# Way down of a SwiGLU block: sums moved from GpSimd to VectorE, seven block products in another order, one operand prepared earlier, LayerNorm rows without GpSimd sums

## The chip, the cores and the metric

The kernel runs on one core of one Trainium2 chip. The metric is the device time of one execution in microseconds; the time before is the median of three runs, 1489.16 us (1487.93 to 1490.58). About 0.2% of it, 3 us, is what such a measurement can tell apart.

## The reference

One encoder layer on x of 1024 tokens by 1024 channels, in float32. A projection gives q, k and v of two attention branches (eight heads each of width 64) and two gates; the branches are projected, gated, summed and projected again, and a LayerNorm follows. What the change touches is the end:

```
x   = layer_norm(ALPHA * x + mix, ln1_g, ln1_b)
gu  = x @ w_ffn_in                 # 1024 x 5632: halves g and u of 2816 columns
g,u = split(gu)
ffn = (silu(g) * u) @ w_ffn_out    # the way up gives h = silu(g)*u, 1024 x 2816; this is the way down
x   = layer_norm(ALPHA * x + ffn, ln2_g, ln2_b)
```

layer_norm takes mean and variance over the 1024 channels of a token and applies gain and bias.

## The kernel before, in words

**Arithmetic.** Every float32 operand of a matmul is split in a high part (rounded to the format that TensorE takes, a ScalarE copy, line 106) and a low part (the rest, a VectorE subtract, line 107); a product is three matmuls: high by high, high by low, low by high (`mm3`, `product`, `triple`).

**Seven products.** Both ways of the feed-forward block use the Strassen-Winograd scheme: an operand is cut in 2 x 2 blocks, and seven block products replace eight, at the price of sums of blocks. On the way up a block of columns f (22 of them, 128 columns each of g and u) takes seven products of 12 matmuls, 84 in all, in the order 1, 2, 6, 5, 7, 3, 4 (`pair_steps`). A product that continues another is accumulated onto the same PSUM bank after ScalarE has copied what stood there (lines 185, 194, 198).

**The way up's last steps.** `up_steps` takes the results: `gt` is the tile with the gate half "11" and the half "22", `h` is the tile of the block's result. Line 846 and 851 apply Silu, 848 and 852 multiply. After an odd block, `left_sums` forms the left operands of the way down for the pair (f-1, f): four sums on GpSimd (lines 821 to 824), and seven stores of 128 x 512 to scratch in HBM (`left_dr`, line 827).

**The way down.** For each of the seven products (the order is in `ORDER`) there are 11 steps, one for each pair; a step loads a left operand (`load`, line 905), splits it (`split_left`), splits a right operand from the rows of w_ffn_out (`split_right`), and runs 12 matmuls, three on each of four banks (`triple`, line 945). The right operands that are sums of blocks are formed in place by `right_sums`, on GpSimd (lines 912, 915, 916, 918). `feed` asks for loads nine steps ahead, sums four ahead, splits three ahead. Two sets of four banks alternate: X (three tr and pv) and Z (two mm, two sc). After a product's last step `take` adds its banks to the accumulators `acc_t` on VectorE (lines 951, 953), which start from x1 (loaded at line 977). Product 4 comes last and runs bank by bank, so that one row of 128 tokens after the other is done; its left and right operands are split during product 3.

**The last LayerNorm.** `end_row` calls `layer_norm` for 128 tokens: statistics (744, 745), variance plus epsilon (746), the power -1/2 on GpSimd (747), centring and gain on VectorE (748). Then, where `quick` is false, ScalarE scales (755) and GpSimd adds the bias (756); where it is true, VectorE does both in two halves (751). Of the last LayerNorm only row 7 is quick. The result goes out by line 957.

**What sets the order.** The source gives an order of emission. The framework's planner places every engine's instructions at build time: an instruction goes onto its engine's queue when, by the planner's estimate, its operands and a buffer are ready, the earlier emitted first among those that are ready. Engines then run their queues in that order and wait for each other by semaphores. Nearly all DMAs are issued on SP's queue. Buffers of 128 x 1024 come from tags with a fixed number of slots (`SLOTS`): yt has 3 (gate tiles, h of odd blocks and of blocks 0 and 2), bw 9 (h of later even blocks, weights, later rows of w_ffn_out), op 8, gt 3 (weights and, on the way down, left operands two to a slot), kp and pt 4 each, xt 16, and qs, kh, kl, v two each, taken in turn (`QKV`). A new tile takes any slot of its tag that is free in the plan, and waits if there is none.

Of the kernel before, what the change touches and what calls it, by code (L numbers as in the profile page):

```python
# [11 lines left out]
F32 = mybir.dt.float32  # L12
# [6 lines left out]
P = 128  # L19
# [9 lines left out]
ORDER = (1, 2, 6, 5, 7, 3, 4)  # L29
# [3 lines left out]
HW = 512  # L33
# [15 lines left out]
def hybrid_trunk_kernel(ctx: ExitStack, tc, x, xt, w_in, b_gate, rel_bias, w_proj,  # L49
# [51 lines left out]
    left_dr = {(p, i): dr.tile([P, HW], F32, name=f"left_dr{p}_{i}")  # L101
# [714 lines left out]
    def left_sums(i):  # L816

        ha, hb = h_of.pop(2 * i), h_of.pop(2 * i + 1)
        sa, sb = slot("op", f"sa{i}"), slot("op", f"sb{i}")
        add = nc.gpsimd.tensor_tensor  # L820
        add(sb[:, LO], ha[:, LO], ha[:, HI], ALU.subtract)  # L821
        add(sa[:, LO], ha[:, HI], hb[:, HI], ALU.add)  # L822
        add(sa[:, HI], sa[:, LO], ha[:, LO], ALU.subtract)
        add(sb[:, HI], hb[:, LO], sa[:, HI], ALU.subtract)
        for p, t in ((1, ha[:, LO]), (2, hb[:, LO]), (4, hb[:, HI]), (5, sa[:, LO]),
                     (6, sa[:, HI]), (7, sb[:, LO]), (3, sb[:, HI])):
            dma(left_dr[p, i], t)

    def up_steps(f):
# [14 lines left out]
        def done(name, acc):  # L844
# [4 lines left out]
            elif name == "21":  # L849
# [3 lines left out]
                if f % 2:  # L853
                    left_sums(f // 2)
# [36 lines left out]
    raw_l, t2, ops = {}, {}, {}  # L891
    xbank, zbank = [], []
# [5 lines left out]
    def load(s):  # L898
        p, i = steps[s]
        if p in (1, 2):  # L900
            load_rows(p - 1, i)
# [5 lines left out]
    def right_sums(s):  # L907
        p, i = steps[s]
        tt = nc.gpsimd.tensor_tensor
        a, b = rows[0][i], rows[1][i]  # L910
        if p == 2:
            tt(a[:, LO], a[:, HI], a[:, LO], ALU.subtract)
        elif p == 6:
            t = t2[i] = slot("kp", f"t2_{i}")[:, LO]
            tt(t, b[:, HI], a[:, LO], ALU.subtract)
            tt(b[:, LO], b[:, LO], t, ALU.subtract)
        elif p == 5:
            tt(a[:, HI], b[:, HI], a[:, HI], ALU.subtract)

    first_tags = iter([("kp",)] * 4)  # L920
    wide = iter([("pt",)] * 4 + [("kp",)] * 4 + [("bw",)] * 3)
# [6 lines left out]
    def split_left(s):  # L928
        p, i = steps[s]
        tags = next(wide) if p == 4 else next(first_tags, QKV)  # L930
        ops["l", s] = split_to(tags, f"dl{p}_{i}", raw_l.pop((p, i)))

    def split_right(s):
        p, i = steps[s]
        a, b = rows[0][i], rows[1][i]
        src = {1: lambda: a[:, LO], 2: lambda: b[:, LO], 6: lambda: t2.pop(i), 5: lambda: a[:, LO],
               7: lambda: a[:, HI], 3: lambda: b[:, HI], 4: lambda: b[:, LO]}[p]()
        tags = ("xt",) if p == 4 else next(first_tags, QKV)
# [103 lines left out]
```

## Time and profile before

| what | value |
|---|---|
| median of the runs | 1489.16 us (1487.93 to 1490.58) |
| profiled execution, its own time | 1487.28 us |
| its span, first to last instruction | 1485.5 us |
| granted TensorE clock | 0.994 |
| way up, matmuls of line 168 | 822.6 to 1255.9 us |
| way down, matmuls of line 945 | 1255.8 to 1471.6 us |
| last store ends | 1485.5 us |

In the profile PE is TensorE's matmuls, PEld its weight loads, DVE is VectorE, ACT ScalarE, POOL GpSimd, SP the queue that issues DMAs. A row of a timeline gives the start, the duration, the engine, the line, what is written and read, how many instructions are merged, and in brackets the idle time of that engine just before and what ended it. A row of groups gives the busy time, the mean nanoseconds of one, then the idle time before them.

### The profile page before, as it was taken

The page shows a single profiled execution, that of the slowest core. Times are in us where ns is not written, and L with a number is a line of the kernel's source. Part 1 is how long each engine was busy: PE and PEld are TensorE (multiplying, and loading weights), DVE is VectorE, ACT ScalarE, POOL GpSimd, SP SyncE. Part 2 cuts the span into 40 slices and gives each one's busy share as a digit, 9 for nine tenths or more (in the row PEclk, how much of TensorE's full clock was granted, in tenths as well). Part 3 has the DMA queues.
Part 4 walks back from the last instruction along what each step waited for, and adds up shares of the span by engine and source line. Part 5 has one row for each costly group of instructions (what it writes and reads, how often), then busy time and mean ns, then how long its engine had stood idle before and what let it go on. Part 6 is the DMA issues. An engine that isn't in the chain of part 4 may idle for free.

```text
span 1485.5 us, 19020 instructions
## 1 busy us (share of the span) xinstructions
PE 1434.5 (97%) x6728; PEld 1176.0 (79%) x6728; DVE 997.1 (67%) x1575; ACT 689.2 (46%) x1222; POOL 391.3 (26%) x384
## 2 busy tenths in 40 slices
PE   8999999999999999999999799999999999999996
PEld 6788888887777888777888588888888888778875
DVE  8865556277677767786948976555555544796757
ACT  6444444376676666864403443333333332434532
POOL 0000000243346546850004121111111113771007
PEclk9999999999999999999999999999999999999998
DMA  6555544756554355748601143333222227843232
GB/s 213 158 183 171 170 149 162 228 167 174 156 156 129 125 145 177 218 168 278 223 15 72 57 140 129 107 106 101 98 91 98 101 101 255 327 134 120 93 100 113
DMA packets 75167, 219.41 MB, mean 148 GB/s; under 512 B 9392, under 2 KB 9392, under 8 KB 75072
## 3 DMA queue, kind: packets, MB, share of 16 engines
q1 hardware_dynamic: 75072, 218.19, 45.4%
q8 instruction: 53, 0.87, 0.2%
q14 instruction: 42, 0.34, 0.1%
HBM read 149.71 MB, written 68.45 MB: 147 GB/s over the span
## 4 chain that ended last, share of the span: by engine, by line
PE 72%; DVE 11%; DMA 5%; POOL 4%; issue 4%; ACT 3%; SPq 1%; DVEq 0%; POOLq 0%; ACTq 0%
PE sxf L168 14%; PE dn L945 10%; PE sxp L168 9%; PE szf L168 7%; PE gps L415 6%; PE szp L168 5%; PE syf L168 3%; PE syp L168 2%; PE ops L116 2%; PE ops L114 2%; PE tp_b L553 2%; PE ops L113 2%; PE yAps L603 2%; DVE kp_b L530 1%; PE tp_a L553 1%
## 5 line engine op out<-in xcount | busy, mean ns | idle before, releaser
L945 PE MATMUL dn<-dr,dl 128*128 128x512 f32 x924 | 213.0, 391 | 2.8 <-DVE dl L107 1.8
L945 PEld LDWEIGHTS dn<-dr,dl 128*128 128x128 f32 x924 | 172.3, 188 | 43.4 <-DVE dl L107 4.6
L532 POOL TENSOR_TENSOR w_b<-w_b,kp_b 128x511 f32<-128x511 f32 (+3 forms) x96 | 99.3, 1039 | 61.6 <-DVE kp_b L530 37.0
L107 DVE TENSOR_TENSOR dl<-raw,dl 128x512 fp32r<-128x512 f32 x77 | 68.7, 904 | 33.6 <-ACT dl L106 33.3
L106 ACT CAST dl<-raw 128x512 fp32r<-128x512 f32 x77 | 47.3, 623 | 83.4 <-PE dn L945 67.2
L747 POOL TENSOR_TENSOR mv<-mv,neghalf 128x1 f32<-128x1 f32 x16 | 23.3, 1454 | 237.2 <-DVE mv L746 233.2
L530 DVE TENSOR_TENSOR_SCAN kp_b<-kp_b,ident_ps 128x384 f32<-128x384 f32 (+6 forms) x88 | 78.5, 892 | 4.6
L415 PE MATMUL gps<-xh,wl_g 128*128 128x512 f32 x192 | 80.3, 418 | 0.0
L415 PE MATMUL gps<-xh,wh_g 128*128 128x512 f32 x192 | 80.3, 418 | 0.0
L415 PE MATMUL gps<-xl,wh_g 128*128 128x512 f32 x192 | 80.3, 418 | 0.0
L476 POOL MEMSET bias<- 64x64 f32 x8 | 1.2, 146 | 275.2 <-ACT bias L475 275.2
L821 POOL TENSOR_TENSOR sb<-h 128x512 f32<-128x512 f32 x11 | 18.9, 1720 | 205.1 <-PE syf L168 131.6
L497 POOL TENSOR_SCALAR w_a<-w_a,st_a 128x640 f32<-128x640 f32 (+2 forms) x64 | 46.4, 728 | 81.8 <-DVE st_a L496 69.0
L522 ACT ACTIVATE kp_b<-sc_b 128x512 f32<-128x512 f32 (+3 forms) x96 | 48.3, 503 | 42.1 <-PE sc_b L459 33.4
L107 DVE TENSOR_TENSOR dr<-rows,dr 128x512 fp32r<-128x512 f32 x66 | 55.4, 847 | 16.1 <-ACT dr L106 16.0
L107 DVE TENSOR_TENSOR pt_b<-tp_b,pt_b 128x512 fp32r<-128x512 f32 (+1 forms) x96 | 51.1, 542 | 17.6 <-ACT pt_b L106 17.4
L168 PE MATMUL szf<-x1S63h,wcf 128*128 128x512 f32 x176 | 57.8, 389 | 0.0
L106 ACT CAST pt_b<-tp_b 128x512 fp32r<-128x512 f32 (+1 forms) x96 | 47.7, 497 | 21.2 <-PE tp_b L553 21.1
L822 POOL TENSOR_TENSOR sa<-h,h 128x512 f32<-128x512 f32 x11 | 17.5, 1589 | 145.0 <-PE sxf L168 105.5
L106 ACT CAST pt_a<-tp_a 128x512 fp32r<-128x512 f32 (+1 forms) x96 | 40.4, 424 | 27.2 <-PE tp_a L553 26.5
L494 ACT ACTIVATE w_a<-w_a,st_a 128x640 f32<-128x640 f32 (+2 forms) x64 | 44.6, 699 | 17.2 <-DVE st_a L489 16.4
L553 PE MATMUL tp_b<-ident,w_b 128*128 128x128 f32 x288 | 48.2, 274 | 4.1 <-DVE pt_b L107 1.8
(1541 smaller groups left out, 4276.7 us busy)
## 6 DMA issues: line engine op xcount, KB each, us to landing
raw<-left_dr SPq DMA_DIRECT2D x77, 256.0 KB, 2.9
wLf<-in_w_ffn_in_dram SPq DMA_DIRECT2D x22, 512.0 KB, 3.8
wRf<-in_w_ffn_in_dram SPq DMA_DIRECT2D x22, 512.0 KB, 4.2
rows<-in_w_ffn_out_dram SPq DMA_DIRECT2D x22, 512.0 KB, 6.7
left_dr<-h SPq DMA_DIRECT2D x33, 256.0 KB, 2.0
v_dr<-v SPq DMA_DIRECT2D x16, 512.0 KB, 3.5
kl<-k_dr SPq DMA_DIRECT2D x32, 256.0 KB, 6.1
v<-v_dr SPq DMA_DIRECT2D x16, 512.0 KB, 3.3
```

Of the source, the lines that this page charges most:

```text
L106: nc.scalar.copy(dst_h, src)
L107: nc.vector.tensor_tensor(dst_l, src, dst_h.bitcast(F32), ALU.subtract)
L113: mm(acc, lh, rh, start=(i == 0), stop=False)
L168: mm(acc, lw[:, ks], rx, start=(first and kt == i == 0), stop=(kt == 3 and i == 2), skip_group_check=not first)
L415: mm(acc, lw[:, ks], rx[k][:, cs], start=(k == j == 0), stop=(k == KT - 1 and j == 2))
L494: nc.scalar.activation(s[:, 0:w], s[:, 0:w], AF.Exp, bias=st[:, m:m + 1], scale=-1.0, accum_out=st[:, 2:3])
L497: nc.gpsimd.tensor_scalar(s[:, 0:w], s[:, 0:w], st[:, 3:4], 0.0, ALU.mult, ALU.add)
L522: nc.scalar.activation(kp[:, c0:e], sc[:, 0:n], AF.Sigmoid, scale=-1.0)
L530: nc.vector.tensor_tensor_scan(kp[:, s0:e], kp[:, s0:e], ident_ps()[:, 0:e - s0], kp[:, s0 - 1:s0], ALU.mult, ALU.bypass)
L532: nc.gpsimd.tensor_tensor(be[:, m0:e], be[:, m0:e], kp[:, m0 - 1:e - 1], ALU.mult)
L553: tr(tp[:, (qb - lo_q) * P:(qb - lo_q + 1) * P], wt[qb - q0][:, (kb - qb) * P:(kb - qb + 1) * P], ident)
L945: mm(acc, lw, rx, start=(first and n == 0), stop=(last and n == 2), skip_group_check=steps[s][0] not in (1, 2, 5))
```

## The change

Four things change in the way down, and one at the end of each pair of blocks on the way up.

- The order of products becomes 5, 1, 3, 6, 2, 7, 4. Products 5, 1 and 2 begin fresh banks; 3 continues 5's banks, 6 continues 1's, 7 continues 6's and 4 continues 7's. Products 5, 3 and 2 use the first set (tr, tr, tr, pv), products 1, 6, 7 and 4 the second (mm, mm, sc, sc).
- The right sums are formed by VectorE in place: one for product 5, two for product 3 and one (`last_sum`) for product 4, emitted during product 2. Before, GpSimd formed four, for products 2, 6 and 5.
- The left operand of product 4 is split at the end of the way up: ScalarE copies the high part into the lower half of the odd block's gate tile, GpSimd subtracts, writing the low part over the value in the tile h; both halves are stored, and the way down loads them as one tile of 128 x 1024 (`load_last`, during product 6) that needs no split. The right operand of product 4 is split during product 7.
- Every row of the last LayerNorm is quick. Rows 0 and 1 are emitted during product 7 (steps 6 and 9), rows 2 and 3 during the first two quarters of product 4, rows 4 to 7 after their quarter as before.
- The takes of a product are emitted one for each of the steps 1 to 4 of the next product instead of all at its end; the loads of x1 are emitted at step 4 of the first product instead of ahead of it; the first operands use the tags of QKV and not kp.

The diff, cut to its core:

```diff
-ORDER = (1, 2, 6, 5, 7, 3, 4)
+ORDER = (5, 1, 3, 6, 2, 7, 4)
...
-    def left_sums(i):
+    def left_sums(i, t):
         ha, hb = h_of.pop(2 * i), h_of.pop(2 * i + 1)
         sa, sb = slot("op", f"sa{i}"), slot("op", f"sb{i}")
-        add = nc.gpsimd.tensor_tensor
-        add(sb[:, LO], ha[:, LO], ha[:, HI], ALU.subtract)
-        add(sa[:, LO], ha[:, HI], hb[:, HI], ALU.add)
-        add(sa[:, HI], sa[:, LO], ha[:, LO], ALU.subtract)
-        add(sb[:, HI], hb[:, LO], sa[:, HI], ALU.subtract)
-        for p, t in ((1, ha[:, LO]), (2, hb[:, LO]), (4, hb[:, HI]), (5, sa[:, LO]),
-                     (6, sa[:, HI]), (7, sb[:, LO]), (3, sb[:, HI])):
-            dma(left_dr[p, i], t)
+        tt = nc.gpsimd.tensor_tensor
+        hi = t[:, LO].bitcast(F32R)
+        nc.scalar.copy(hi, hb[:, HI])
+        tt(sa[:, LO], ha[:, HI], hb[:, HI], ALU.add)
+        tt(sb[:, LO], ha[:, LO], ha[:, HI], ALU.subtract)
+        tt(sa[:, HI], sa[:, LO], ha[:, LO], ALU.subtract)
+        tt(sb[:, HI], hb[:, LO], sa[:, HI], ALU.subtract)
+        tt(hb[:, HI].bitcast(F32R), hb[:, HI], t[:, LO], ALU.subtract)
+        for p, src in ((1, ha[:, LO]), (2, hb[:, LO]), (5, sa[:, LO]), (6, sa[:, HI]),
+                       (7, sb[:, LO]), (3, sb[:, HI])):
+            dma(left_dr[p, i], src)
+        for cs, src in ((LO, t[:, LO]), (HI, hb[:, HI])):
+            dma(left_dr[4, i][:, cs], src)
...
-                    left_sums(f // 2)
+                    left_sums(f // 2, tl["t"])
...
     def right_sums(s):
         p, i = steps[s]
-        tt = nc.gpsimd.tensor_tensor
+        tt = nc.vector.tensor_tensor
         a, b = rows[0][i], rows[1][i]
-        if p == 2:
-            tt(a[:, LO], a[:, HI], a[:, LO], ALU.subtract)
-        elif p == 6:
-            t = t2[i] = slot("kp", f"t2_{i}")[:, LO]
-            tt(t, b[:, HI], a[:, LO], ALU.subtract)
-            tt(b[:, LO], b[:, LO], t, ALU.subtract)
-        elif p == 5:
+        if p == 5:
+            t1[i] = slot("kp", f"t1_{i}")[:, LO]
+            tt(t1[i], a[:, HI], a[:, LO], ALU.subtract)
+        elif p == 3:
             tt(a[:, HI], b[:, HI], a[:, HI], ALU.subtract)
+            tt(a[:, LO], a[:, HI], a[:, LO], ALU.add)
+
+    def last_sum(i):
+        a, b = rows[0][i], rows[1][i]
+        nc.vector.tensor_tensor(b[:, LO], b[:, LO], a[:, LO], ALU.subtract)
...
+    def load_last(i):
+        t = ops["l", base[4] + i] = slot(next(wide), f"dl4_{i}", F32R)
+        dma(t.bitcast(F32), left_dr[4, i])
...
     def end_row(tt):
-        layer_norm(acc_t[tt], *norm2, f"2_{tt}", tt == 7,
+        layer_norm(acc_t[tt], *norm2, f"2_{tt}", True,
...
+        if p == 5 and i == 4:
+            for tt in (4, 5, 6, 7, 0, 1, 2, 3):
+                dma(acc_t[tt], x1_dr[tt])
...
+        if left and i >= 1:
+            take(*left.pop(0))
+        if p == 6:
+            load_last(i)
+        if p == 2:
+            last_sum(i)
+        if p == 7:
+            split_right(base[4] + i)
+            if i == 0:
                 norm2 = [bcast(src, slot("yt", f"ln2{n}"))
                          for src, n in ((ln2_g, "g"), (ln2_b, "b"))]
+            if i in (6, 9):
+                end_row((6, 9).index(i))
+        for mt in range(4):
+            triple(sets[p][mt], s, mt, i == NP2 - 1)
+        if i == NP2 - 1:
+            t0, half, first = takes[p]
+            left = [(t0 + mt, half, sets[p][mt], first) for mt in range(4)]
+    while left:
+        take(*left.pop(0))
     for mt in range(4):
         for i in range(NP2):
-            triple(xbank[mt], base[4] + i, mt, False, i == NP2 - 1)
-        take(4 + mt, LO, xbank[mt], True)
+            triple(sets[4][mt], base[4] + i, mt, i == NP2 - 1)
+        if mt < 2:
+            end_row(2 + mt)
+        take(4 + mt, LO, sets[4][mt], True)
         end_row(4 + mt)
```

More of the change, by code (lines that the diff above doesn't have):

```diff
@@ L968, in feed @@
     def feed(s):
[L969 to L977 removed]
+        for d in range(SPLITS + 1):
+            advance("load", min(s + LOADS, base[4] - 1), load)
+            advance("sums", s + d + 1, right_sums)
+            advance("l", min(s + d, base[4] - 1), split_left)
+            advance("r", min(s + d, base[4] - 1), split_right)
```

78 lines of the change are left out of this document (30 added, 48 removed).

## The prediction

> **What bounds the kernel now.** I read the page first, then the way down product by product, then the matmul rows, then the tail, and last the start of the way up, where the change adds work.
>
> ```profile
> span 1485.5 us, 19020 instructions
> PE 1434.5 (97%) x6728; PEld 1176.0 (79%) x6728; DVE 997.1 (67%) x1575; ACT 689.2 (46%) x1222; POOL 391.3 (26%) x384
> ```
>
> TensorE is nearly always busy, so only two things pay: time in which it waits, and time after its last matmul. The table by stretches shows the way down. Its columns are the stretch, its length, then busy time and count of PE, PEld, DVE, ACT and POOL, the clock, and DMA. The products of the old order are 1, 2, 6, 5, 7, 3, 4; shown are the first three, the sixth (product 3) and the last (product 4).
>
> ```profile
> 1255.80:1285.80 30.00, 30.00 (x133) 24.68 (x132) 16.96 (x17) 8.94 (x15) 20.92 (x15) 1.00 0.83 311
> 1285.80:1320.70 34.90, 32.07 (x133) 24.23 (x132) 34.51 (x31) 13.85 (x25) 29.35 (x18) 1.00 0.66 230
> 1320.70:1350.60 29.90, 29.90 (x133) 24.77 (x132) 27.93 (x33) 12.60 (x22) 17.11 (x12) 1.00 0.32 97
> ...
> 1410.50:1441.50 31.00, 31.00 (x133) 24.23 (x132) 18.82 (x31) 15.39 (x27) 0.00 (x0) 1.00 0.37 119
> 1441.50:1471.60 30.10, 30.09 (x133) 24.59 (x131) 26.99 (x39) 5.77 (x5) 21.77 (x11) 1.00 0.19 78
> ```
>
> Each product is 132 matmuls. Five stretches take 29.9 to 30.1 us; product 2 takes 34.9 and product 3 takes 31.0. In product 2 VectorE is busy for 34.51 of 34.90 us and GpSimd for 29.35. The next rows are the matmuls themselves (the first from the chain of waits, for the pace, the second from the groups by line, the rest from the timeline).
>
> ```profile
> 1040.41 2.72 PE szf L168 x12
> L945 PE MATMUL dn<-dr,dl 128*128 128x512 f32 x924 | 213.0, 391 | 2.8 <-DVE dl L107 1.8 <-DVE dr L107 1.0
> 1255.78 33.43 PE L945 MATMUL dn<-dr,dl 128*128 128x512 f32 x146
> 1289.50 3.01 PE L945 MATMUL dn<-dr,dl 128*128 128x512 f32 x12 [0.29 <-DVE dl L107]
> 1292.90 3.02 PE L945 MATMUL dn<-dr,dl 128*128 128x512 f32 x12 [0.40 <-DVE dl L107]
> ...
> 1309.90 161.69 PE L945 MATMUL dn<-dr,dl 128*128 128x512 f32 x707 [0.38 <-DVE dr L107]
> ```
>
> Twelve matmuls undisturbed take 2.72 us, 0.2267 each, so 924 need 209.5 us. They run from 1255.78 to 1309.90 + 161.69 = 1471.59, and the last one shows its own 0.39 instead of 0.23, so 215.65 us is the time to set against that. TensorE loses **6.15 us** on the way down. From 1289.50 to 1309.90 one step of twelve follows the other after 3.40 us, and VectorE's low half (line 107) ends each wait. Why VectorE is late:
>
> ```profile
> 1296.17 1.78 DVE L107 TENSOR_TENSOR dr<-rows,dr 128x512 fp32r<-128x512 f32 x1
> 1297.37 1.74 POOL L916 TENSOR_TENSOR rows<-rows,t 128x512 f32<-128x512 f32 x1
> 1297.87 1.78 DVE L107 TENSOR_TENSOR dl<-raw,dl 128x512 fp32r<-128x512 f32 x1
> ...
> 1312.07 0.68 DVE L107 TENSOR_TENSOR dl<-raw,dl 128x512 fp32r<-128x512 f32 x1
> 1312.67 0.68 DVE L107 TENSOR_TENSOR dr<-rows,dr 128x512 fp32r<-128x512 f32 x1
> ```
>
> The same subtract takes 0.68 us and follows its predecessor after 0.60 where GpSimd is idle, and takes 1.78 and follows after 1.70 where GpSimd adds in between. Two per step make the 3.40 us. So VectorE is full of waiting, not of work.
>
> The tail, from the last matmul on:
>
> ```profile
> 1471.63 0.69 DVE L951 SCALAR_TENSOR_TENSOR x<-x,dn 128x512 f32<-128x512 f32 x1 [0.34 <-PE dn L945]
> 1472.35 0.69 DVE L744 BATCH_NORM_STATS2 bn<-x 128x6 f32<-128x512 f32 x1
> 1473.46 2.92 DVE L748 SCALAR_TENSOR_TENSOR x<-x,mv,ln2g 128x1024 f32<-128x1024 f32 x1
> 1475.26 1.53 POOL L747 TENSOR_TENSOR mv<-mv,neghalf 128x1 f32<-128x1 f32 x1
> ...
> 1478.05 2.34 POOL L756 TENSOR_TENSOR x<-x,ln2b 128x1024 f32<-128x1024 f32 x1 [1.26 <-ACT x L755]
> 1480.34 0.55 POOL L747 TENSOR_TENSOR mv<-mv,neghalf 128x1 f32<-128x1 f32 x1
> 1480.93 1.42 DVE L751 SCALAR_TENSOR_TENSOR x<-x,mv,ln2b 128x512 f32<-128x512 f32 x2 [4.55 <-POOL mv L747]
> ```
>
> The last row's sums are ready at 1473.46, but its power (line 747) starts at 1480.34 only: GpSimd is still at the powers and bias sums (line 756) of earlier rows.
>
> **The change, part by part.** *Right sums to VectorE.* 44 GpSimd adds leave the way down, 44 VectorE adds of the same shape come in, at the 0.60 us spacing above. Per step of 2.72 us VectorE then has, in the new order 5, 1, 3, 6, 2, 7: 3, 2, 4, 2, 3 and 3 operations, at most 2.40 us. Four takes of 0.69 come on top in each product but the first, in product 3 making 11 x 2.40 + 2.8 = 29.2 us against 29.9. They are hidden by the matmuls and by operands split three steps (8.2 us) ahead; without that cover, at the full 0.68, product 3 would lose 11 x 2.72 + 2.8 - 29.9 = 2.8 us. Product 2's loss goes in full: bounds of the gain are 0 and 5.0, I take 5.0, because nothing is left on GpSimd there.
>
> *Last product's operands made on the way up.* In old product 3, 11 casts and 11 subtracts for product 4's left side share the step with its own; there 1.1 us are lost. They go. Instead there are per pair of column blocks one ScalarE copy, one GpSimd subtract and one more store, and eleven loads of 512 KB in place of 256 KB on a way down whose DMA share is 0.3 after the second product. I take the whole 1.1 as gain (bounds 0 and 1.1), with the above 6.15 in all.
>
> What these operations cost on the way up:
>
> ```profile
> L106 ACT CAST dl<-raw 128x512 fp32r<-128x512 f32 x71 | 43.7, 623 | 80.9 <-PE dn L945 67.2 <-DMA raw<-left_dr 10.3 <-DVE dl L107 2.3
> 881.82 0.59 ACT L194 COPY h<-sxf 128x512 f32<-128x512 f32 x1 [1.01 <-DVE h L852]
> 883.57 2.20 POOL L823 TENSOR_TENSOR sa<-sa,h 128x512 f32<-128x512 f32 x1
> 884.16 0.39 PE L168 MATMUL sxf<-x1S57h,waf2h 128*128 128x512 f32 x1
> 914.77 0.59 ACT L185 COPY gt<-sxf 128x512 f32<-128x512 f32 x1 [0.95 <-DVE h L852]
> 916.52 1.30 POOL L823 TENSOR_TENSOR sa<-sa,h 128x512 f32<-128x512 f32 x1
> 917.24 0.39 PE L168 MATMUL sxf<-x1S63h,wbf4h 128*128 128x512 f32 x1
> ```
>
> The copy (0.62, as the cast of that size) waits for VectorE's product of line 852; behind it on ScalarE stands the next block's copy of line 185, which ends at 914.77 + 0.59 = 915.36 and is needed at 917.24. The 0.62 fits in the 1.88 us. The subtract (1.30) lengthens GpSimd's chain; the stores behind it on SP stand before weights that are used a block, 19 us, later. No price there.
>
> But the gate tile, which used to be free after line 852, is now held until the subtract. Tag yt has three slots, and at two places all three are held. At 881.82 line 194 writes h of block 2 at once after line 852, into the slot of block 1's gate tile. After the change the first slot free is that of h of block 0, when line 823 ends: 883.57 + 2.20 = 885.77. With its own 0.59 the copy ends at 886.4, and the matmul of 884.16 that accumulates on the copied bank is late by **2.2 us**, unless TensorE's order gets other matmuls first. At 914.77 it is the same with block 4's gate tile: free at 916.52 + 1.30 = 917.82, copied at 918.4, late by **1.2 us**. Later even blocks write h into tag bw, and a slot is free. Bounds 0 and 3.4; I take 1.5, since ready matmuls of other products stand beside both places, but the order in which they run isn't shown.
>
> At the end of the way up the last pair's four remaining GpSimd operations (some 6 us) fall into the first product, as three plus line 912's sums do now without a loss (20.92 us of GpSimd in that stretch): 0, at most 1.
>
> *Loads that move.* The eight loads of x1 go from the start of the way down to the first product's fifth step, past the first operands on SP; the second half of w_ffn_out goes from the second product to the third.
>
> ```profile
> 1265.61 4.38 SPq L977 DMA_DIRECT2D x<-x_dr  x8
> ```
>
> Today they stand before later left operands, and line 106 waits 10.3 us for those (row above) without a loss on TensorE. Moved back they are needed at the first take, some 20 us later: no price, no gain.
>
> *LayerNorm without GpSimd sums.* Rows 0 to 6 lose ScalarE's scaling and the bias sum, and get line 751 as row 7 has it. The nearest row is that of the first LayerNorm, where it ran so:
>
> ```profile
> 824.43 1.27 DVE L748 SCALAR_TENSOR_TENSOR acc<-acc,mv,ln1g 128x1024 f32<-128x1024 f32 x1
> 824.66 1.46 POOL L747 TENSOR_TENSOR mv<-mv,neghalf 128x1 f32<-128x1 f32 x1 [4.01 <-DMA x_dr<-acc]
> 826.15 1.41 DVE L751 SCALAR_TENSOR_TENSOR acc<-acc,mv,ln1b 128x512 f32<-128x512 f32 x2 [0.44 <-POOL mv L747]
> ```
>
> Line 751 starts 1.72 us after line 748. In the tail that is 1473.46 + 1.72 = 1475.18 instead of 1480.93: **5.75 us** saved, if VectorE has nothing left from earlier rows. A row on VectorE costs 0.60 (one half's statistics) + 1.11 (1472.35 to 1473.46) + 1.72 + 1.41 = 4.84 us. Rows 0 and 1 go into product 7, where 9.7 + 27 splits (16 of its own, 11 for product 4) at 0.60 + 2.8 = 28.7 us stand against 29.9; rows 2 to 6 and three takes need 24.2 + 2.1 = 26.3 us before the last take, 29.9 after product 4's start. Row 6 starts when the third quarter of 33 matmuls ends, at 22.4, and is done at 22.4 + 0.7 + 4.8 = 27.9, 2 us early. Line 751 waits in VectorE's queue for the power (0.45 of the 1.72); behind it stand splits and takes, covered by the three steps. Without cover, rows 0 and 1 cost up to 4.
>
> *Product 4 right behind 7, on the same banks.* The first take of 7 must end before product 4 may write that bank. The bank is done nine matmuls (2.0 us) early and the take needs 0.69, so it is hidden, if VectorE is free; if the take waits for product 7's last matmul or stands behind a line 748, TensorE waits 0.8 to 2.0. I take 0.5.
>
> **The sum.** The profiled execution has 1487.28 us, 1.8 beside the span. 1487.28 - 6.15 - 5.75 + 1.5 + 0.5 = 1477.4. The median of the runs shown, 1489.16, is 1.9 above that execution, so I forecast 1477.4 + 1.9 = **1479**; with no new wait at all 1477.3.
>
> **Rivals.** *VectorE becomes the bound.* For it: 34.51 of 34.90 us busy in product 2 already. Against: the 0.68 us rows. Price: the uncovered 2.8 in product 3 and 4 in product 7: 1479 + 6.8, about 1485. [...]
>
> *The gate tile is short at every pair (the other side).* If line 185 had to wait for the subtract after each odd block, GpSimd would get there at 916.52 + 3 x 1.37 = 920.6, the copy would end at 921.2, 4.0 us late for 917.24: ten times, 40 us, about 1519. It decides from 1.2 us per pair on, which eats the 11.9. For it: the two waits on line 852 above. Against, from the waits of line 185 over the whole way up:
>
> ```profile
>   PE sxf L168: 22.6, 18
> ```
>
> 18 of its 19 waits end with the matmul and not with a tile, so a slot is free then.
>
> *Only the tail is gained.* If product 2's delay is VectorE's own, the change doesn't do there what it says: 1489.2 - 5.75 + 1 = 1484.5. Against it: the pairs of rows at 1297 and 1312.
>
> *The start of the way down gives it back.* Product 5 has three VectorE operations a step. At 1.70 us each, beside the last pair's GpSimd chain, a step takes 5.1 instead of 2.72, and four steps lose 9.5: 1488.5. For it: only four steps' operands fit in the slots of QKV, where kp held two more. Against: four GpSimd operations delay only some five of VectorE's, and three steps (8.2 us) are ready ahead.
>
> **Chances.** Forecast 0.58, own range 1476 to 1482; VectorE bound 0.14; only the tail 0.12; the start 0.09; slot short at every pair 0.07. About 3 us (0.2%) is what a measurement can tell from no change. Faster 0.84, same 0.09, slower 0.07. The range: the low end is 1477.3 less the 1.2 us that the fastest run shown lies under the median, 1476; the upper end takes in both 1485 rivals: 1485.5.
>
> **What would show it.** Right: no line 107 of 1.7 us on the way down but in its first 12 us; seven stretches of 29.9; the last line 751 some 3.5 us after the last take's start. Wrong: TensorE waiting for line 194 or 185 at more than two places of the way up, for a take at product 4's start, or for line 107 in the new products 3 and 7; a last row that waits for VectorE.

## Result: slower by 2.9%, and all of it on the way up

The changed kernel takes **1532.86 us** (median; 1527.51 to 1534.25) beside 1489.76 us for the kernel before in the same measurement: a ratio of 1.029 (95% interval 1.027 to 1.031). The forecast was 1479 us, in a range of 1476 to 1485.5. The profiled execution took 1533.44 us. Its page begins:

```profile
span 1531.3 us, 18982 instructions
PE 1452.2 (95%) x6728; PEld 1188.7 (78%) x6728; DVE 984.8 (64%) x1622; ACT 679.8 (44%) x1215; POOL 329.6 (22%) x344
```

TensorE has the same 6728 matmuls and is busy for 17.7 us longer, VectorE and GpSimd for less than before. So TensorE waits more, and part of its matmuls are slower. In what follows the line numbers of the changed kernel are used for it: 822 is ScalarE's copy of the high part, 823 to 826 the four old sums (in the new order: sa lower, sb lower, sa upper, sb upper), 827 the new subtract, 830 and 832 the stores, 856 and 857 the Silu and the multiply that were 851 and 852, 955 the matmul of the way down.

First the way up, as one stretch from its first matmul to the way down's first, before and after. The columns are as in the prediction: length, busy time of PE, PEld, DVE, ACT, POOL, clock, DMA.

```profile
822.63:1255.78 433.15, 425.95 (x1875) 349.24 (x1874) 256.74 (x321) 156.29 (x221) 69.44 (x47) 0.99 0.33 115
```

```profile
824.55:1307.73 483.18, 444.24 (x1875) 359.13 (x1873) 253.99 (x325) 159.43 (x227) 76.72 (x51) 0.96 0.31 108
```

That stretch is **50.0 us** longer, and the granted clock in it falls from 0.99 to 0.96. Then the way down, the first two of the seven products in the new order (the other five are as long as the second):

```profile
1307.73:1343.68 35.95, 31.84 (x133) 25.84 (x132) 22.64 (x32) 12.65 (x22) 13.38 (x5) 0.95 0.71 247
1343.68:1373.60 29.92, 29.92 (x133) 24.78 (x132) 27.11 (x46) 12.48 (x22) 0.00 (x0) 1.00 0.95 344
```

Six of seven products run without any loss, as forecast; the first loses 6.0 us, 4.1 of them in one wait, the rest in matmuls at a lower clock (0.95 over that stretch). And the tail, from the take of the last bank:

```profile
1523.40 0.69 DVE L961 SCALAR_TENSOR_TENSOR x<-x,dn 128x512 f32<-128x512 f32 x1 [2.12 <-PE dn L955]
1525.17 1.27 DVE L748 SCALAR_TENSOR_TENSOR x<-x,mv,ln2g 128x1024 f32<-128x1024 f32 x1
1526.88 1.41 DVE L751 SCALAR_TENSOR_TENSOR x<-x,mv,ln2b 128x512 f32<-128x512 f32 x2 [0.44 <-POOL mv L747]
```

Line 751 starts 1.71 us after line 748 (1.72 was forecast). From the last matmul's start to the end of the span there are 8.3 us instead of 14.3.

The whole difference of the two spans, 1531.3 - 1485.5 = 45.8 us, is then: way up 50.0, its start 1.9 later, way down -0.2 (6.15 gained, 6.0 lost anew at its start), tail -6.0.

What TensorE waits for on the way up and at the start of the way down (us in all, times, longest):

```profile
PE sxf L168 <- DVE gt L181: 20.4, 7, 3.8
PE sxf L168 <- ACT h L194: 9.6, 8, 3.3
PE dn L955 <- DVE dr L107: 4.1, 1, 4.1
PE sxf L168 <- ACT gt L185: 2.3, 1, 2.3
```

Line 181 had one wait of 0.2 us before; lines 194 and 185 had none on the way up. In seven of the pairs it happens in the even block that follows (6 to 18); lines 194 and 185 each make TensorE wait once more, in blocks 2 and 4 (the 3.3 and 2.3 of the table). Here is one such place from the timeline, all engines (the pair of blocks 10 and 11 has ended, block 12 is under way):

```profile
1097.45 0.68 DVE L857 TENSOR_TENSOR h<-h,gt 128x512 f32<-128x512 f32 x1
...
1102.49 2.27 POOL L827 TENSOR_TENSOR h<-h,gt 128x512 fp32r<-128x512 f32 x1
1104.72 1.29 POOL L826 TENSOR_TENSOR sb<-h,sa 128x512 f32<-128x512 f32 x1
1106.04 0.32 SPq L830 DMA_DIRECT2D left_dr<-sb  x1
1106.05 0.62 ACT L106 CAST wcf<-wRf 128x512 fp32r<-128x512 f32 x1 [3.42 <-POOL sb L826]
1106.57 0.58 ACT L194 COPY h<-sxf 128x512 f32<-128x512 f32 x1
1107.20 0.50 PE L168 MATMUL sxf<-x1S57h,waf12h 128*128 128x512 f32 x1 [0.91 <-ACT h L194]
1107.91 0.51 SPq L140 DMA_DIRECT2D wRf<-in_w_ffn_in_dram  x1
1114.14 0.69 DVE L143 TENSOR_TENSOR taf<-wRf,wLf 128x512 f32<-128x512 f32 x1 [6.76 <-DMA wRf<-in_w_ffn_in_dram]
1115.36 0.69 DVE L181 TENSOR_TENSOR gt<-sxf,gt 128x512 f32<-128x512 f32 x1
1116.10 0.74 PE L168 MATMUL sxf<-x1A,wbf12h 128*128 128x512 f32 x2 [3.12 <-DVE gt L181]
```

The plan has put the new subtract (827) ahead of the last sum (826), and GpSimd's chain ends at 1106.01. Two things start at that moment: the last store of sb on SP, behind which the next weights are issued, and ScalarE's cast of line 106, which writes a tile in one of the op slots that sa and sb held. Behind the cast stands line 194, and TensorE waits for it (product 7, about 1.07 us in each of seven pairs). The weights are there at 1114.14, and SP asked for them at 1107.91 only, after the stores; VectorE's line 143, which needs them, stands ahead of line 181, and TensorE waits for that (product 4, 2.6 to 3.9 us). In the trace of the whole way up from 860 us on there are 16 waits of over 0.9 us (counted as what the distance of two starts has beyond 0.227), 34.9 us together, and 61 matmuls that start 0.43 us apart instead of 0.227, 12.0 us together: 46.9 of the 50.0. In the kernel before there is no such wait, and one such matmul.

The start of the way down, on VectorE, GpSimd and SP:

```profile
1309.56 7.03 POOL L823 TENSOR_TENSOR sa<-h,h 128x512 f32<-128x512 f32 x1 [30.15 <-DVE h L857]
1316.61 3.73 SPq L830 DMA_DIRECT2D left_dr<-sa  x2
...
1324.34 0.41 SPq L901 DMA_DIRECT2D rows<-in_w_ffn_out_dram  x1
1329.32 0.69 DVE L918 TENSOR_TENSOR t<-rows 128x512 f32<-128x512 f32 x1 [8.78 <-DMA rows<-in_w_ffn_out_dram]
```

The last pair's first sum takes 7.03 us instead of 1.3, while VectorE runs the new right sums and splits back to back; then three of VectorE's operations take 1.67 to 1.78 us beside the rest of the chain. SP holds the pair's stores, and behind them the load of rows, until 1324.34; line 918 waits 8.78 us for it, and TensorE 4.1.

### The profile page after: what moved, and what is told of

Same layout as the page of the kernel before. It is cut to its first block, busy times and chain, and to the rows that moved or that the text cites. A ratio compares the mean times of both kernels' runs of the same rounds, so it can differ in the third digit from the quotient of the medians.

```text
span 1531.3 us, 18982 instructions
## 1 busy us (share of the span) xinstructions
PE 1452.2 (95%) x6728; PEld 1188.7 (78%) x6728; DVE 984.8 (64%) x1622; ACT 679.8 (44%) x1215; POOL 329.6 (22%) x344
## 5 line engine op out<-in xcount | busy, mean ns | idle before, releaser
L106 ACT CAST dl<-raw 128x512 fp32r<-128x512 f32 x66 | 41.0, 623 | 95.6 <-PE dn L955 80.8
L107 DVE TENSOR_TENSOR dl<-raw,dl 128x512 fp32r<-128x512 f32 x66 | 46.4, 704 | 35.0 <-ACT dl L106 34.8
L143 DVE TENSOR_TENSOR taf<-wRf,wLf 128x512 f32<-128x512 f32 x22 | 15.2, 690 | 66.4 <-DMA wRf<-in_w_ffn_in_dram 66.4
L181 DVE TENSOR_TENSOR gt<-sxf,gt 128x512 f32<-128x512 f32 x22 | 15.1, 688 | 64.1 <-PE sxf L168 64.1
L494 ACT ACTIVATE w_a<-w_a,st_a 128x640 f32<-128x640 f32 (+2 forms) x64 | 44.6, 698 | 18.0 <-DVE st_a L489 17.3
```

Source lines behind the costliest of these rows:

```text
L106: nc.scalar.copy(dst_h, src)
L107: nc.vector.tensor_tensor(dst_l, src, dst_h.bitcast(F32), ALU.subtract)
L494: nc.scalar.activation(s[:, 0:w], s[:, 0:w], AF.Exp, bias=st[:, m:m + 1], scale=-1.0, accum_out=st[:, 2:3])
```

## Experiments

All kernels were timed beside the kernel before on the same chip; "way up" is the time from the first to the last start of a matmul of line 168 in the profiled execution: 432.9 us before, 483.0 after.

### e1_old_left: all of the change but the new end of a pair

```diff
# left_sums has again the four sums and the seven stores of before; of what goes:
-        nc.scalar.copy(hi, hb[:, HI])
...
-        tt(hb[:, HI].bitcast(F32R), hb[:, HI], t[:, LO], ALU.subtract)
...
     def load_last(i):
-        dma(t.bitcast(F32), left_dr[4, i])
+        dma(t[:, HI].bitcast(F32), left_dr[4, i])
...
         if p == 2:
             last_sum(i)
+            t = ops["l", base[4] + i]
+            split(t[:, LO], t[:, HI], t[:, HI].bitcast(F32))
```

> The kernel after, but the end of each pair on the way up is the one of before: four sums on GpSimd in the old order, the raw half stored, and the left operand of product 4 split on the way down during product 2. Theory (the new end of each pair is the whole loss): the way up is back to 433 us from its 483, the way down keeps 209.5 to 212 us, the tail stays at 8.3; 1532.9 - 50 = 1479 to 1484. Rival (the loss is the gate tile, the planner or another part of the change): it stays over 1520.

Measured: **1478.32 us** (1477.14 to 1480.47), ratio 0.9928 (0.9912 to 0.9944). The way up is 433.2 us. The first product of the way down:

```profile
1255.55:1286.12 30.57, 30.21 (x134) 24.70 (x132) 22.73 (x33) 12.03 (x21) 10.27 (x3) 1.00 0.73 270
```

It loses 0.65 us; the others lose nothing. So the whole loss on the way up, and 5.4 of the 6.0 us at the start of the way down, come from the new end of a pair: its five GpSimd operations, its copy, its stores and the tile it holds, taken together. Without it the kernel is faster than both. The splits that were moved to the way up fit into product 2 without a loss.

### e3_sb_first, e4_pool_q, e5_low_dve_sb_first: what in the end of a pair

e3 forms the lower half of sb first, as before. e4 issues the stores on GpSimd's own queue. e5 is e3 with the low part on VectorE instead of GpSimd.

```diff
 # e3
-        tt(sa[:, LO], ha[:, HI], hb[:, HI], ALU.add)
         tt(sb[:, LO], ha[:, LO], ha[:, HI], ALU.subtract)
+        tt(sa[:, LO], ha[:, HI], hb[:, HI], ALU.add)
 # e4, all stores of left_sums
-            dma(left_dr[p, i], src)
+            nc.gpsimd.dma_start(left_dr[p, i], src)
...
 # e5, beside e3
-        tt(hb[:, HI].bitcast(F32R), hb[:, HI], t[:, LO], ALU.subtract)
+        nc.vector.tensor_tensor(t[:, HI].bitcast(F32R), hb[:, HI], t[:, LO], ALU.subtract)
...
-        for cs, src in ((LO, t[:, LO]), (HI, hb[:, HI])):
-            dma(left_dr[4, i][:, cs], src)
+        dma(left_dr[4, i], t)
```

> The kernel after, with the lower half of sb formed first, as before, so that GpSimd forms it some 17 us earlier and four of its five operations are left behind line 857. Theory (the length of GpSimd's chain decides, by the stores on SP and the weights behind them): each pair's wait at product 4 falls by 1.3 us of about 3, the wait at product 7 (1.07) goes; 8 pairs at 2.4 us and part of the slow matmuls: 1505 to 1518. Rival (the added store, the copy on ScalarE or the held gate tile decide, whatever the length): within 5 us of 1532.9.

> The kernel after, with the eight stores of each pair issued on GpSimd's own queue instead of SP's. Theory (the weights' loads stand behind the stores on SP, VectorE's line 143 waits for them, line 181 and product 4 behind it): the waits of TensorE for line 181 (20.4 us) and the slow matmuls behind them go, those for line 194 (9.6 us) may stay; 1490 to 1505. Rival (the late GpSimd results hold the slots of sa and sb, and that alone makes ScalarE and VectorE late): the waits for line 181 stay, over 1520.

> The kernel after, with the low part of product 4's left operand formed by VectorE in the upper half of the gate tile (one store of 128x1024 in place of two), and sb's lower half first: GpSimd has the four sums of before in their old order. Theory (GpSimd's chain decides): the way up is back to 433 us, the way down keeps its gain; 1476 to 1482. Rival (VectorE is as tight as GpSimd at that place: one more operation of 0.69 ahead of line 181 makes product 4 late by as much, 8 to 10 times, with slow matmuls behind it): 1486 to 1500. Rival (the copy on ScalarE or the held gate tile decide): over 1520.

Measured: e3 1530.94 us (ratio 1.029, 1.0263 to 1.0317; way up 479.9), e4 1534.61 (1.0293, 1.0258 to 1.0328; 485.6), e5 1492.74 (1.0023, 1.0009 to 1.0037; 445.9).

e5: with the subtract off GpSimd, and sb in the old order, 37 of the 50 us on the way up are back. The 13 that are left are waits of 1.1 to 1.9 us per pair at product 3, and 2.5 us in blocks 2 and 4. The time is in the first rival's range, but the wait is not the rival's: TensorE doesn't wait for line 181. In block 10 the chain ends 5.5 us after the pair's last multiply, near the 5.2 of before, but the store of 128x1024 stands between it and the weights; these are issued at 6.4 us, ScalarE's cast of them starts at 11.2 when they have landed, and line 198 behind it at 12.2 (before: 5.6, 9.3 and 10.3). So the trace points to that store, not to VectorE's subtract.

e3 and e4 missed too: both times are in their rivals' ranges, and their traces say why. In both the waits of product 7 and product 4 are gone, and one wait of 3.6 to 4.8 us stands in their place in blocks 6 to 18, at product 3, for line 198 (ScalarE's copy of product 5's result). In e4, after line 857 at 1052.54:

```profile
1061.04 1.10 POOL L830 DMA_DIRECT2D left_dr<-sa  x2
1064.72 0.62 ACT L106 CAST wcf<-wRf 128x512 fp32r<-128x512 f32 x1 [5.40 <-DMA left_dr<-sa]
1067.14 0.58 ACT L198 COPY gt<-szf 128x512 f32<-128x512 f32 x1
```

SP's queue is free there, and the next weights are issued early, at 1056.48 and 1058.71. But sa keeps its op slot until its store has landed, 3.7 us after its issue, and ScalarE's cast waits 5.40 us for the slot with line 198 behind it. So the queue is not the only tie: the slot is a second one. What it costs alone e4 doesn't show, because GpSimd issues the stores of sa only after its whole chain, 8.5 us after line 857, where SP issued them at 2.1 and 5.1 us in the changed kernel: the slot comes free later than it did there.

For the kernels with the stores on SP, the chain can be read link by link. Before (the pair 10 and 11 ended, block 12 under way), with TensorE not waiting at product 3 (the last two rows are VectorE's and TensorE's at product 4):

```profile
1066.95 0.69 DVE L852 TENSOR_TENSOR h<-h,gt 128x512 f32<-128x512 f32 x1
1070.84 1.30 POOL L824 TENSOR_TENSOR sb<-h,sa 128x512 f32<-128x512 f32 x1
1072.58 0.38 SPq L127 DMA_DIRECT2D wLf<-in_w_ffn_in_dram  x1
1076.26 1.05 ACT L106 CAST wlf15h<-wLf 128x1024 fp32r<-128x1024 f32 x1 [2.21 <-issue]
1077.22 0.58 ACT L198 COPY gt<-szf 128x512 f32<-128x512 f32 x1
1078.18 0.69 DVE L143 TENSOR_TENSOR taf<-wRf,wLf 128x512 f32<-128x512 f32 x1 [3.89 <-DMA wRf<-in_w_ffn_in_dram]
1081.46 0.73 PE L168 MATMUL sxf<-x1A,wbf12h 128*128 128x512 f32 x2 [0.23 <-DVE gt L181]
```

e3, the same one pair earlier (8 and 9 ended, block 10 under way):

```profile
1048.27 0.69 DVE L857 TENSOR_TENSOR h<-h,gt 128x512 f32<-128x512 f32 x1
1053.43 2.27 POOL L826 TENSOR_TENSOR sb<-h,sa 128x512 f32<-128x512 f32 x1
1057.10 0.40 SPq L127 DMA_DIRECT2D wLf<-in_w_ffn_in_dram  x1
1062.60 1.04 ACT L106 CAST wlf13h<-wLf 128x1024 fp32r<-128x1024 f32 x1 [5.77 <-DMA wRf<-in_w_ffn_in_dram]
1063.56 0.58 ACT L198 COPY gt<-szf 128x512 f32<-128x512 f32 x1
1064.19 0.80 PE L168 MATMUL szf<-x1S63h,wcf 128*128 128x512 f32 x1 [4.25 <-ACT gt L198]
```

Counted from the start of the pair's last multiply (line 852 or 857), the chain's end, the issue of the left weights, ScalarE's cast of them and line 198 stand at 5.2, 5.6, 9.3 and 10.3 us before, and at 7.4, 8.8, 14.3 and 15.3 us in e3. So of 5.0 us more, 2.2 are the chain, 1.0 the two stores more between it and the weights, and 1.8 the load itself, which is now used 5.5 us after its issue instead of 3.7, with three stores ahead of it instead of one.

### b1_double, b4_double_first, b7_no_op: the chain's end in the kernel before

Three kernels from the one before. b1 repeats the last GpSimd sum, b4 the first, b7 is b1 with sa in the gate tile and the upper half of sb in the even block's h.

```diff
 # b1
         add(sb[:, HI], hb[:, LO], sa[:, HI], ALU.subtract)
+        add(sb[:, HI], hb[:, LO], sa[:, HI], ALU.subtract)
 # b4
         add(sb[:, LO], ha[:, LO], ha[:, HI], ALU.subtract)
+        add(sb[:, LO], ha[:, LO], ha[:, HI], ALU.subtract)
 # b7, g is the odd block's gate tile
+        add(g[:, LO], ha[:, HI], hb[:, HI], ALU.add)
+        add(g[:, HI], g[:, LO], ha[:, LO], ALU.subtract)
+        add(ha[:, HI], hb[:, LO], g[:, HI], ALU.subtract)
+        add(ha[:, HI], hb[:, LO], g[:, HI], ALU.subtract)
...
```

> The kernel before, with the last of the four GpSimd sums (line 824) done twice: the same values, one more GpSimd operation of 128x512 at the end of each pair's chain, nothing on another engine. Theory (the end of GpSimd's chain is tied to TensorE without slack, by the slots of sa and sb and by the stores ahead of the next weights): some 1.3 to 2.2 us late at 8 pairs, with or without slow matmuls behind it: 1500 to 1535. Rival (the chain has slack of its own; ScalarE's copy, the added store or the held gate tile made the loss): within 3 us of 1489.

> The kernel before, with the first of the four GpSimd sums (line 821) done twice: as much more GpSimd work as in b1_double, but at the early end of the chain, some 17 us ahead of the other three. Theory (what counts is when the chain ends): within 2 us of 1489, the way up 433 us. [...]

> b1_double with its late results out of the op slots: sa goes into the odd block's gate tile and the upper half of sb into the even block's h; only the early lower half of sb stays in op. The chain on GpSimd and the stores on SP's queue are as long as there. If the op slots make the loss: ScalarE's cast no longer waits for line 825, the way up falls from 451 to 433 us and some 3 us for blocks 2 and 4, whose gate tile is held longer: 1490 to 1495. If the stores ahead of the weights on SP's queue make it: the waits at product 3 stay at 1.6 to 1.8 us, the way up at 448 to 455: 1505 to 1515.

Measured: b1 **1509.88 us** (ratio 1.0139, 1.0115 to 1.0163; way up 450.8), b4 1493.37 (1.0031, 1.002 to 1.0041; 435.1), b7 1517.74 (1.0199, 1.0182 to 1.0215; 454.6).

One more GpSimd sum at the end of the chain costs 20 us in a kernel in which nothing else is changed; the same sum at its early end costs 4 by the medians. b4's profiled execution took 1489.48 us, 3.9 under its median; it has one wait of 1.9 us in block 2 and none in later blocks, and what the other executions lose it doesn't show. b4 is 2 us over the theory's range and 16.5 us below b1. So in these two kernels it is the moment at which the chain ends that counts, and not how much GpSimd has to do. b1's links after the pair 8 and 9, whose last multiply (line 853 there) starts at 1041.02:

```profile
1046.27 2.15 POOL L825 TENSOR_TENSOR sb<-h,sa 128x512 f32<-128x512 f32 x1
1048.87 0.39 SPq L127 DMA_DIRECT2D wLf<-in_w_ffn_in_dram  x1
1052.70 1.04 ACT L106 CAST wlf13h<-wLf 128x1024 fp32r<-128x1024 f32 x1 [3.13 <-issue]
1053.65 0.58 ACT L198 COPY gt<-szf 128x512 f32<-128x512 f32 x1
1054.28 0.50 PE L168 MATMUL szf<-x1S63h,wcf 128*128 128x512 f32 x1 [1.66 <-ACT gt L198]
```

Line 198 starts 12.6 us after that, 2.35 later than before, and TensorE waits 1.8; in e3 it was 5.0 later and the wait 4.4. So the kernel before had about **0.6 us** in hand at this place, and each microsecond beyond is paid in full, at seven or eight pairs. In e5, where the store and not the chain makes line 198 late, the same holds: 1.9 us later, a wait of 1.4.

b7 took longer than either of its expectations. The waits at product 3 are gone in all pairs: the plan, which the edit changes too, issues the right weights ahead of the stores, and line 143 runs at 1047.02, 1.6 us after the pair's last multiply and not 13.0 as in b1. But h of the even block now keeps its slot of tag bw for the late store, the next line 194 waits for that slot, and TensorE waits 1.3 us per pair at product 7:

```profile
1054.78 0.58 ACT L194 COPY h<-sxf 128x512 f32<-128x512 f32 x1 [0.31 <-DMA left_dr<-h]
```

Blocks 2 and 4, whose gate tile is held longer, cost 3.1 and 4.1 us on top, and the start of the way down waits 5.6 us for a cast of line 106, which wasn't followed further. So b7 doesn't tell the op slots from the stores ahead of the weights; it shows a third tie of the same kind. In these runs a late result makes whoever needs its buffer next late, whether the buffer is of tag op, yt or bw.

### e8_copy: the rest of the new end, without its subtract

```diff
# against e1_old_left
         ha, hb = h_of.pop(2 * i), h_of.pop(2 * i + 1)
+        nc.scalar.copy(t[:, LO].bitcast(F32R), hb[:, HI])
...
             dma(left_dr[p, i], src)
+        dma(hi_dr[i], t[:, LO])
```

> The kernel e1_old_left, and with it the rest of the new end of a pair but its subtract: ScalarE's copy of the high part into the gate tile, the tile held for it, and its store (the copy is stored and not used). Theory: of the 13 us that e5_low_dve_sb_first still loses on the way up, blocks 2 and 4 have 2.5 (held tile) and the rest is VectorE's subtract beside GpSimd's chain: the way up 433 to 436, 1478 to 1482. Rival (the copy ahead of line 185 on ScalarE, or the eighth store, costs a microsecond per pair): 1486 to 1492.

Measured: 1486.6 us (ratio 0.9987, 0.9975 to 0.9999), 8 us above e1; the way up is 439.9 us, 6.8 above e1. Blocks 2 and 4 wait 1.3 and 1.24 us, as in e5; block 14 waits 1.2 us at product 4, and four places in blocks 12 to 16 wait 0.3 to 0.5. The rival is nearer: the copy, the held tile and the eighth store are not free either. No run has the copy or the store alone, but the trace shows what the store does: in block 10 the chain ends at 5.2 us as before, the left weights behind the added store are issued at 6.1 and not 5.6, and line 198 starts at 11.0, 0.7 later. That is about what was in hand.

### e6_fill: the slow matmuls

```diff
+            if nm[0] == "f" and int(nm[1:]) % 2 == 0 and int(nm[1:]) >= 6:
+                product(bank("tr", f"fill{nm}"), W, ops, 7, True)
             product(st["sz"], W, ops, 3, False)
```

> The kernel e3_sb_first with 12 matmuls more ahead of product 3 of each even block from 6 on, a repetition of product 7 into a bank that nobody reads: 8 x 2.72 = 21.8 us more work for TensorE, in the place where it waits 3.6 to 4.6 us with its clock at half speed after it. Theory (the slow matmuls, 2.6 us per pair, come from the idle time ahead of them): the wait left is 1 to 2 us, the matmuls behind it run at 0.227 us, 7 x 2.6 us less and one block where there was no wait 2.7 more: 1512 to 1518. Rival (they are slow for another reason, operands or contention): no gain, 1531 to 1550.

Measured: **1523.72 us** (1519.96 to 1524.23), between the two expectations: 7 us less than e3 with 21.8 us more work for TensorE. The stretch just before the first matmul of product 3 in block 10, and the one behind it, in e3:

```profile
1060.00:1064.10 4.10, 0.00 (x0) 0.00 (x0) 0.28 (x1) 1.50 (x3) 0.00 (x0) 0.75 0.74 295
1064.20:1070.00 5.80, 5.80 (x16) 4.62 (x17) 4.44 (x7) 0.88 (x1) 0.00 (x0) 0.60 0.02 9
```

and in e6:

```profile
1058.00:1062.60 4.60, 3.20 (x15) 2.31 (x13) 0.26 (x1) 1.47 (x3) 0.00 (x0) 1.00 0.88 294
1062.80:1068.60 5.80, 5.80 (x26) 4.78 (x27) 5.80 (x9) 1.14 (x2) 0.00 (x0) 1.00 0.03 8
```

After 4 us without a matmul, 5.8 us hold 16 matmuls at a granted clock of 0.60; after a wait that is mostly filled, 26 at 1.00, with VectorE busier than in e3. From 860 to 1250 us the granted clock is 0.96 in e3 and 1.00 in e6. On the whole way up e3 has 54 slow matmuls (10.6 us) and e6 one; e3 waits 33.1 us in its waits of over 0.9 us, e6 15.8. The theory's mechanism holds; the gain was 7 and not 13 to 19 us, because the slow spells of e3 cost 10.6 us in all, 1.5 per pair (I had taken 2.6), the filling takes 21.8 us and saves only 17.3 of waiting, and block 20 had no wait to fill.

### b2_ln, b3_sums, b9_both: the two terms of the gain, alone and together

```diff
 # b2
-        layer_norm(acc_t[tt], *norm2, f"2_{tt}", tt == 7,
+        layer_norm(acc_t[tt], *norm2, f"2_{tt}", True,
 # b3, right_sums, in the old order of products
-        tt = nc.gpsimd.tensor_tensor
+        tt = nc.vector.tensor_tensor
 # b9: both
```

> The kernel before, with all rows of the last LayerNorm quick and nothing else. The prediction's term: 5.75 us less, 1483.4. Rival (VectorE has left-over work in the tail): 1485 to 1489.

> The kernel before, with the right sums of the way down on VectorE, in the old order of products, and nothing else. The prediction's term: product 2 loses its 4.9 to 5.0 us no longer, 1484.3. Rival (VectorE is the bound there): no gain, 1488 or above.

> The kernel before, with the right sums on VectorE and all rows of the last LayerNorm quick, both in the old order of products: what the change is worth without its new order and without the new end of a pair. Theory (the order matters: with the old one rows 0 to 3 of the LayerNorm stand at product 4's start and leave VectorE behind in the tail, and the left operand of product 4 is split during product 3): 6.0 and 2.7 less than before, 1480.5, the tail at 10.8 us and 1.1 us lost in product 3. Rival (the order is worth nothing): as e1_old_left, 1478.3, the tail at 8.3.

Measured: b2 1486.72 us (ratio 0.9987, 0.9976 to 0.9999), b3 1483.37 (0.9965, 0.9952 to 0.9979), b9 1482.45 (0.996, 0.9946 to 0.9973). b3's products 2 and 3:

```profile
1286.83:1316.75 29.92, 29.92 (x134) 24.78 (x133) 28.05 (x47) 12.70 (x22) 0.00 (x0) 1.00 0.70 241
1406.51:1437.63 31.12, 31.05 (x133) 24.23 (x132) 18.93 (x31) 15.39 (x27) 0.00 (x0) 1.00 0.37 118
```

Product 2 goes from 34.90 to 29.92 us with VectorE doing more of the work: 47 operations in 28.05 us, where 31 took 34.51 beside GpSimd's 29.35 us of sums. It was the neighbour on GpSimd that made it late. Product 3 keeps its 1.2 us, as the prediction had it for the splits of product 4.

b2 earns 2.7 us by the medians (its interval is 0.1 to 3.6 us), not 5.75. The profiled execution took 1489.22 us: its way up starts 5.6 us later than before, behind code that is the same, so only its tail is read here:

```profile
1475.67 1.29 PE L945 MATMUL dn<-dr,dl 128*128 128x512 f32 x5
1477.80 0.68 DVE L951 SCALAR_TENSOR_TENSOR x<-x,dn 128x512 f32<-128x512 f32 x1
1482.48 1.42 DVE L751 SCALAR_TENSOR_TENSOR x<-x,mv,ln2b 128x512 f32<-128x512 f32 x2 [0.44 <-POOL mv L747]
```

The last take starts 0.84 us after the end of the last matmul (1475.67 + 1.29) and not 0.04 as before (1471.59, 1471.63), because VectorE is still busy with row 6: in the old order the first four rows stand at the start of product 4, and VectorE does not catch up. The tail, from the last matmul's start, is 10.9 us. With the new order it is 8.3 (the changed kernel, e3, e8); in e1's profiled execution the last line 751 starts as early as there, but the span ends 1.6 us later. b9 keeps both marks of the old order (tail 10.9, 1.0 us lost in product 3) and is 4 to 5 us above e1, by the medians and by the ratios (0.996 and 0.9928). It is 2 us above what the theory gave and 4 above the rival: the new order, with the places that it gives to rows and takes, is worth something.

## Why the prediction was wrong

**The step that failed** is this one, of the added subtract: "The subtract (1.30) lengthens GpSimd's chain; the stores behind it on SP stand before weights that are used a block, 19 us, later. No price there." The chain was seen, the queue behind it too, and the price was left at nothing without following who waits for the weights first. It is not TensorE, a block later: it is ScalarE's cast (line 106) and VectorE's line 143, 9.3 and 11.2 us after the pair's last multiply in the kernel before, and behind each of them on its queue stands a copy or a sum (lines 198 and 181) that TensorE needs in the present block. The runs put in its place: 0.6 us in hand, a chain that ends 8.6 us after the start of the pair's last multiply (1097.45 to 1106.01) and not 5.2 (some 2.2 more by the subtract, forecast at 1.30, and 1.2 by the lower half of sb, which the new order of the sums makes late), two stores more behind it, some 4 us of waiting per pair (1.07 at product 7 and 2.6 to 3.9 at product 4), and, behind most of the longer ones, a granted clock of 0.52 to 0.70 for 3.5 us. The profile of before held the warning (rows above): the wait of 0.23 us for line 181 in block 12 and the 3.89 us that VectorE stands idle behind a load of wRf. The prediction has neither row. A wait above zero, however short, says that at this place nothing is in hand.

**The rival with the right sign** was "the gate tile is short at every pair", 1519 us. Its price was near (40 us, where the way up lost 50), but that is chance, because its mechanism is not what happened: line 185 waits once (2.3 us), in block 4, and from block 6 on a slot is free, as the argument against it said. The sign that the prediction gave for being wrong, TensorE waiting for line 194 or 185 at more than two places, came true for line 194. What was missing among the rivals is the same lateness by the other buffers and queues: the op slots of sa and sb, the weights behind the stores. Its threshold, 1.2 us per pair, was passed by far.

**The gate tile at blocks 2 and 4**: forecast 2.2 and 1.2 us late, taken at 1.5 in all. In the changed kernel they were 3.4 and 2.5 us; with the chain of before (e5, e8) 1.3 and 1.24. The mechanism was right, the escape ("ready matmuls of other products stand beside both places") was not: TensorE took none.

**Right sums on VectorE, -6.15**: right where it is undisturbed. Six products run at 29.92 us in the changed kernel, and in e1 the seven lose 0.65 us in all. b3 shows product 2's part alone, 4.98, so the rival "only the tail is gained" fell. Product 3 in the new order with its four operations a step is 29.92 too, so VectorE is not the bound, and the rival of 1485 us fell. Product 2 takes 34.90 us with the sums on GpSimd and 29.92 with them on VectorE (before and b3).

**The operands of product 4 made on the way up**: the 1.1 us is saved, but e1 saves it as well without making anything on the way up, by splitting during product 2. The step bought nothing and carried the whole loss.

**The start of the way down**, forecast "0, at most 1", and as a rival up to 9.5 us by VectorE at 1.70 us an operation. It was 6.0 us, 5.4 of them from the new end of a pair (e1). It isn't VectorE at 1.70 us an operation: ten of its operations keep their 0.60 while GpSimd's first sum stands for 7.03 us, three are slowed behind that, and then VectorE is idle for 8.78. The loss comes through SP, where the load of rows stands behind the last pair's stores.

**Tail, -5.75**: measured 6.0. The condition in the text, "if VectorE has nothing left from earlier rows", is what the new order supplies: b2, without it, gets 3.4 of it in its trace.

**The take between 7 and 4, +0.5**: nothing; product 4 follows with no gap.

Without the step that failed the sum was good: "with no new wait at all 1477.3", and e1, which has almost none, takes 1478.32.

## What to carry to other kernels

Before adding an operation to a chain on an engine with much idle time, follow its last result through every tie it has: the buffers it holds until its stores have landed, the loads queued behind those stores, the instructions queued behind whoever needs these loads; and look for the smallest wait of the bottleneck at that place, because 0.2 us of waiting means that nothing is in hand there. A change made of several parts is worth timing part by part: here one part that earned nothing cost 54 us and hid the 11 us of the others. Where a wait can't be removed at once, matmuls that do nothing can be tried: in e6 21.8 us of them gained 7 us, and the granted clock behind the wait was 1.00 and not 0.60.

## What the runs showed of the hardware that was not expected

**The clock after a wait.** Of the waits on the way up, those of 1.05 to 1.07 us in the changed kernel and those up to 1.9 us in b1, e5 and e6 leave TensorE at full speed: the first matmul behind the wait takes 0.34 us, the next ones 0.227, and the granted clock from 860 to 1250 us is 1.00 in each of these three. Of the nine waits of 2.5 to 3.9 us in the changed kernel eight are followed, at once or a few matmuls later, by six to eight matmuls at 0.43 us or near it, with a granted clock of 0.52 to 0.70 in the 3.5 us behind the wait; in e3 two stretches of 5.8 us behind a wait have 0.50 and 0.60. The ninth, of 2.9 us in block 16 (1203.77), is followed by full speed and a clock of 1.00, while those of 2.5 us in blocks 4 and 14 (927.87, 1159.81) are followed by 0.68 and 0.70. So it isn't the length of the wait alone that decides here; what else does isn't shown. The slow matmuls made 12.0 of the 50 us.

**GpSimd beside a stream of VectorE operations.** In the prediction's rows the two alternate, 1.7 us each. At the start of the way down VectorE's sums and splits come back to back, 0.60 us apart, and GpSimd's sum, started at 1309.56, ends only at 1316.6, while ten of VectorE's keep to 0.68 us each and only the eleventh takes 1.67; e1 shows the same 7.03 us beside ten. In e5 the sum takes 8.24 us beside twelve. The same sum took 1.29 us in the kernel before (line 822, 1261.17). Why the two alternate at one place and GpSimd stands at the other isn't shown.

**A load behind stores.** A load of 512 KB on SP's queue was used 3.7 us after its issue with one store of 256 KB just ahead of it (before), 3.8 in b1, 4.0 with two of them ahead (e8), 4.8 with one of 256 and one of 512 KB (e5), and 5.5 with three of 256 (e3), all in block 10 or 12. No run changes the stores and nothing else, so that the stores are the reason is argued and not shown.
